# Three early gate/up product groups moved in between the last rows of an out-projection

## The chip, the cores and the metric

The kernel runs on one core of one Trainium2 chip. The metric is the device time of one execution in microseconds (us), smaller is better. Engines are called TensorE (PE in the profile, its weight loads PEld), VectorE (DVE), ScalarE (ACT), GpSimd (POOL) and SyncE (SP, here the queue that issues the DMAs).

## The reference

A bidirectional encoder trunk with two layers of width 1024 over 1040 tokens (1024 and 16 learned ones ahead of them, which are dropped at the end), all in float32. Cut to what matters:

```
for each layer:
    h  = x + hybrid_mixer(rmsnorm(x)) @ w_out      # chunked gated DeltaNet heads and a gated convolution
    g, u = split(rmsnorm(h) @ w_gate_up)           # the gate/up products
    x  = h + (silu(g) * u) @ w_down
return rmsnorm(x)
```

## The kernel before

The data lie transposed, features on the 128 partitions and tokens along the free axis, so a residual of 1024 features is eight "rows" m = 0 to 7 of 128 features. A float32 product is made of three matmuls on values split into a high and a low half (high by high, high by low, low by high). ScalarE makes the high half by a copy (`hi`), VectorE or GpSimd the low one by a subtraction (`lo`). The work is written with a scheduler that fixes the order on each engine from an estimate of durations and from priorities; tiles come from pools with few buffers (raw weights: 2, split weights `whi`/`wlo`: 3; PSUM banks `acc` 3, `f` 2, `b` 2, `a` 1), so an instruction may also wait until a buffer is given back.

Around the change, each layer runs so:

**Out-projection, second part.** `out_part(z, m)` makes row m for one half of the tokens, first z = 0 (the two middle quarters), then z = 1 (the two outer quarters). It loads 256 KB of `w_out` (raw, L129), splits it (L130 on ScalarE, L131), runs 12 matmuls into each of two PSUM banks (L157 to L159), reads each bank out into the residual on VectorE (`add_h`, L905), squares the row for the norm (L949 on ScalarE, L950 adds it to `rstd`), and stores the row (L952 on SyncE, where the store waits for L905).

**The tiles of the FFN.** Gate and up are made by a Strassen-like scheme with seven products of half the size per group f, on sums of the residual over the two token halves. The tiles B11 and B21 hold the normed middle tokens and are ready when the z = 0 rows are. T1, B22, T2, T3 and T4 need the z = 1 rows too: between and behind those rows VectorE makes the sums (L977, L1001) and, with ScalarE, the splits (`t_split`: L964 the high half on ScalarE, L965 the low one on VectorE; `t_split_w`: L177 and L178). T2 and T3 take the place of the tiles that every out-projection matmul reads, and T4 that of a residual row group, whose other half later holds a ring of weights.

**Early products.** Behind the rows, for f = 0 to 3, one loop makes the first products of f, from B11 (into `u`) and, added to it, from B21 (into `g`): two raw loads (L1087, L1088), two weight splits (`w_op`: L1042 on ScalarE, L1043 on GpSimd), matmuls (`prod`: L1060 to L1062), and a copy out of PSUM on ScalarE after each (L1095, L1098). They read only B11 and B21. A product with one of the two is a half group here, and (f, q) names it: q = 0 with B11, q = 1 with B21. In layer 0 a half group has 24 matmuls with 260 columns in two banks, in layer 1 (1024 tokens) 12 with 512 columns in one bank.

**Then** `finish_bc` (L207 to L215) sums the squares over the partitions and makes the norm, and the main loop over f loads the weights (L1278 to L1281), makes their sums on VectorE (L1286 to L1291), and runs the other products: P5 and its readers (L1310), the gate (L1321, L1324), P7 (L1328) and P4 (L1337), to the last factor (L1351 to L1354).

Of the kernel before, what the change touches and what calls it, by code (L numbers as in the profile page):

```python
# [7 lines left out]
F32 = mybir.dt.float32  # L8
F32R = mybir.dt.float32r
BF16 = mybir.dt.bfloat16  # L10
AF = mybir.ActivationFunctionType
ALU = mybir.AluOpType
# [3 lines left out]
KT = 8  # L16
# [13 lines left out]
P_L = 65  # L30
P_N1, P_N2, P_CV, P_SC, P_DN = 0, 8, 16, 52, 64
# [11 lines left out]
def trunk(ctx: ExitStack, tc: tile.TileContext, xT, w_in, w_ba, w_out, w_gu, w_dn,  # L43
          par_d, alog_d, dtb_d, cst_d, eye_d, out):
    nc = tc.nc
    sb = ctx.enter_context(tc.tile_pool(name="sb", bufs=1))
# [5 lines left out]
    def nm(p):  # L52
        cnt[0] += 1
        return f"{p}_{cnt[0]}"

    def big(tag, dt=F32):
        return sb.tile([128, 4, L], dt, tag=tag, name=nm(tag))

    def row(tag, dt=F32, bufs=1):
        return sb.tile([128, L], dt, tag=tag, bufs=bufs, name=nm(tag))  # L60
# [4 lines left out]
    def c4k(tag="c"):  # L65
        return sb.tile([128, L], F32, tag="c", bufs=2, name=nm(tag))

    def bank(tag):
        return psp.tile([128, 512], F32, tag=tag, bufs={"acc": 3, "a": 1, "f": 2, "b": 2}[tag], name=nm("p" + tag))
# [29 lines left out]
    act = nc.scalar.activation  # L99
    tt = nc.vector.tensor_tensor  # L100
    stt = nc.vector.scalar_tensor_tensor
    ts = nc.vector.tensor_scalar
    ptt = nc.gpsimd.tensor_tensor
    dma = nc.sync.dma_start
# [4 lines left out]
    par = sb.tile([128, P_W], F32, name="par")  # L109
# [170 lines left out]
    for l in range(DEPTH):  # L280
        last = l == DEPTH - 1
        X, Y = S[l % 2], S[1 - l % 2]
        pcol = lambda c: par[:, l * P_L + c:l * P_L + c + 1]
# [147 lines left out]
        P0 = [sb.tile([16, 4, 16], F32, tag=f"P0{d}", name=nm("P0")) for d in range(2)]  # L431
# [195 lines left out]
        for pos, i in enumerate(seq):  # L627
# [16 lines left out]
            if pos == 2:  # L644
                g, negG, nGb, negE, gl, bkd = gates()
# [232 lines left out]
        for i, (d, s) in enumerate(order):  # L878
            at_prio(base - 17000 + 4000 * (1 - d) + 400 * s)
            c = s if d == 0 else 8 - s  # L880
# [6 lines left out]
        hb = [big(X[0][0]), big(X[0][1])]  # L887
# [15 lines left out]
        def add_h(m, then=None):  # L903
            def f(ps, n0, n1):
                tt(out=hr[m][:, n0:n1], in0=ps, in1=hr[m][:, n0:n1], op=ALU.add)  # L905
                if then is not None:
                    then(n0, n1)
            return f
# [32 lines left out]
        def out_part(z, m):  # L941
            dense(wload(w_out[l, m, :, 0:4, :], 4), os_, hcut[z], add_h(m), pwide)

            v, sv = half(hr[m][:, o0:L], z), half(ss[:, o0:L], z)
            if m == 0:
                act(out=sv, in_=v, func=AF.Square)
            else:
                sq = c4k("sq")[:, 0:NB].rearrange("p (g e) -> p g e", g=2)
                act(out=sq, in_=v, func=AF.Square)  # L949
                (ptt if z == 1 and m % 2 == 0 else tt)(out=sv, in0=sv, in1=sq, op=ALU.add)  # L950
            for (n0, n1) in hcut[z]:
                dma(hd[m][:, n0:n1], hr[m][:, n0:n1])  # L952
# [3 lines left out]
        def t_tile(tag):  # L956
            t = big(tag, F32R).rearrange("p a (b e) -> p (a b) e", b=2)
            return t[:, 0:4, 0:NB], t[:, 4:8, 0:NB]

        def t_split(T, src, z, k0):  # L960

            hi, lo = (t[:, k0:k0 + 2, :].rearrange("p k (g e) -> p k g e", g=2) for t in T)
            s = half(src[:, k0:k0 + 2, o0:L], z)
            act(out=hi, in_=s, func=AF.Copy)  # L964
            tt(out=lo, in0=s, in1=hi.bitcast(F32), op=ALU.subtract)  # L965

        def hx(k, z):
            return half(hr[k][:, o0:L], z)

        def t_split_w(T, k, z):  # L970

            hi, lo = (t[:, k % 4, :].rearrange("p (g e) -> p g e", g=2) for t in T)
            split_scaled(hx(k, z), pcol(P_N2 + k), hi, lo)

        def t_sum(k, z, src, col, other, op=ALU.subtract):

            stt(out=hx(k, z), in0=src, scalar=col, in1=other, op0=ALU.mult, op1=op)  # L977

        npar = sb.tile([128, 4], F32, tag="npar", name=nm("npar"))
        ts(out=npar, in0=par[:, l * P_L + P_N2:l * P_L + P_N2 + 4], scalar1=-1.0, scalar2=None, op0=ALU.mult)  # L980
        X0, X1 = hb
        T = {}

        for m in range(KT):
            out_part(0, m)
            if m > 0:
                if m in (1, 5):
                    T[("B11", "B21")[m // 4]] = t_tile((Y[0][0], X[0][2])[m // 4])
                t_split_w(T[("B11", "B21")[(m - 1) // 4]], m - 1, 0)
        for m in range(KT + 2):  # L990
            if m < KT:
                out_part(1, m)
            if m == 0:
                t_split_w(T["B21"], 7, 0)
            k = m - 2
            if k < 0:
                continue
            if k < 4:
                if k == 0:
                    T["T1"] = t_tile(Y[0][2])  # L1000
                ts(out=hx(k, 1), in0=hx(k, 1), scalar1=pcol(P_N2 + k), scalar2=None, op0=ALU.mult)  # L1001
                t_sum(k, 0, hx(k, 0), npar[:, k:k + 1], hx(k, 1), ALU.add)
                if k % 2:
                    t_split(T["T1"], X0, 0, k - 1)
            else:
                c = pcol(P_N2 + k)
                if k == 4:
                    T["B22"] = t_tile(Y[0][1])
                t_split_w(T["B22"], k, 1)
                t_sum(k - 4, 1, hx(k, 1), c, hx(k - 4, 1))  # L1010
                t_sum(k, 1, hx(k, 1), c, hx(k - 4, 0))
                t_sum(k, 0, hx(k, 0), c, hx(k, 1))
        T["T2"] = t_tile("P0")
        T["T3"] = t_tile("P1")
        for k in (0, 2):
            t_split(T["T2"], X1, 1, k)
        for k in (0, 2):
            t_split(T["T3"], X0, 1, k)
        T["T4"] = t_tile(X[0][0])
        for k in (0, 2):  # L1020
            t_split(T["T4"], X1, 0, k)


        ad = dram.tile([FT, 128, L], F32, name=nm("ad"))
        ring = [None]
        wn = [0]
# [11 lines left out]
        def w_op(src, early=False):  # L1038
            hi, lo = wslot(early)
            n = src.shape[1]  # L1040
            hi, lo = hi[:, 0:n, :], lo[:, 0:n, :]
            act(out=hi, in_=src, func=AF.Copy)  # L1042
            ptt(out=lo, in0=src, in1=hi.bitcast(F32), op=ALU.subtract)  # L1043
            return hi, lo
# [3 lines left out]
        def pbank():  # L1048
            bn[0] += 1
            return bank(("acc", "f", "acc", "b", "acc", "f", "b", "a")[bn[0] % 8])  # L1050

        CW = E if E * 4 > 1024 else NB
        NJ = NB // CW

        def prod(ps, w, t, j, first, stop=True):
            nk = w[0].shape[1]
            for k in range(nk):
                cs = slice(CW * j, CW * j + CW)
                th, tl = (t[0][k], t[1][k]) if isinstance(t[0], list) else (t[0][:, k, :], t[1][:, k, :])
                mm(ps[:, :CW], w[0][:, k, :], th[:, cs], start=first and k == 0, stop=False, skip_group_check=True)  # L1060
                mm(ps[:, :CW], w[0][:, k, :], tl[:, cs], start=False, stop=False, skip_group_check=True)  # L1061
                mm(ps[:, :CW], w[1][:, k, :], th[:, cs], start=False, stop=stop and k == nk - 1, skip_group_check=True)  # L1062

        def raw4(tag):
            if tag == "raw":
                return wp.tile([128, WK, 128], F32, tag="raw", bufs=2, name=nm("raw"))
            return t2k("rw")

        def part(t, z, j):

            v = half(t[:, o0:L], z)
            return v[:, j, :] if NJ == 2 else v
# [6 lines left out]
        def pin(ps):  # L1079
            return loc(ps, 0)  # L1080


        NE = 4
        early = {}
        for f in range(NE):
            A11, A12 = raw4("raw"), raw4("raw")
            dma(A11, w_gu[l, f, 0, :, 0:4, :])  # L1087
            dma(A12, w_gu[l, f, 0, :, 4:8, :])  # L1088
            w1, w2 = w_op(A11, True), w_op(A12, True)
            g, u = (row(Y[1], F32, 3), row(X[1], F32, 3)) if f < 3 else (row(Y[1] + "f"), c4k())  # L1090
            early[f] = g, u
            ab = [pbank() for j in range(NJ)]
            for j in range(NJ):
                prod(ab[j], w1, T["B11"], j, True)
                act(out=part(u, 0, j), in_=pin(ab[j]), func=AF.Copy)  # L1095
            for j in range(NJ):
                prod(ab[j], w2, T["B21"], j, False)
                act(out=part(g, 0, j), in_=pin(ab[j]), func=AF.Copy)  # L1098

        finish_bc(ss, o0, L, rsd[0])  # L1100

# [149 lines left out]
        for t in range(4, NP * 7):  # L1251
            u = max(0, 4 * (t // 3 - 1) - 1 + t % 3)
# [23 lines left out]
        for f in range(FT):  # L1276
            A11, A12, A21, A22 = raw4("raw"), raw4("raw"), raw4("ck2"), raw4("ck2")
# [20 lines left out]
            g, u = early[f] if f < NE else (row((X[1], Y[1])[f % 2] + "f"), row(X[1], F32, 3))  # L1298
# [65 lines left out]
        hb = [big(X[0][0]), big(X[0][1])]  # L1364
# [38 lines left out]
        for i in range(NF):  # L1403
            u = (42, 44, 46, 70)[i]
            under[u - 3].append(lambda i=i: plain_load(i))
            under[u].append(lambda i=i: plain_row(i))
        for u, (p, b, m) in enumerate(UNITS):
            if b == 1 and p in FIRST:
                dh, z = FIRST[p]
                q = 4 * dh + m  # L1410
# [163 lines left out]
```

## Time and profile before

| | us |
|---|---|
| median of 3 runs | 2555.83 (2554.69 to 2557.81) |
| profiled execution | 2552.45 |
| its span in the trace | 2550.7 |
| mean granted TensorE clock | 0.997 |

All numbers of the trace come from the profiled execution. A row of a timeline gives the start in us from the span's start, the length, the engine, the line and operation, out<-in with tile names (buffer numbers left out), the shape, and in brackets the time for which the engine had been idle ahead of it and what ended that. A row of the table by stretches gives for each engine the busy time within the stretch with the count of instructions, then the TensorE clock that was granted (1.00 is full), the mean busy share of the DMA engines and GB/s. Layer 0 passes the end of its out-projection at about 600 us, layer 1 at about 1863 us.

### The profile page before, as it was taken

The numbers are of one execution on the slowest core, as the hardware profiler recorded it, in microseconds if no ns is written. First come the engines' busy times: TensorE is split into PE (matmuls) and PEld (weight loads), VectorE is DVE, ScalarE is ACT, GpSimd is POOL, SyncE is SP. The second block draws the span as 40 slices with busy tenths as digits, with TensorE's granted clock in tenths as the row PEclk, the third lists the DMA queues.
The fourth block names the chain that finished last, engine by engine and source line by source line (L and its number), as shares of the span: only waits on it lengthen the run. The fifth ranks groups of instructions, "written<-read, shape, count | busy, mean of one in ns | idle before, by whom it ended". The sixth has DMA issues, their size and how long they took to land. (4 is left out here: it accounts for less than half of the span.)

```text
span 2550.7 us, 45276 instructions
## 1 busy us (share of the span) xinstructions
PE 2488.7 (98%) x17508; PEld 2276.4 (89%) x17508; DVE 1613.0 (63%) x2442; ACT 1070.3 (42%) x2053; POOL 1141.9 (45%) x885
## 2 busy tenths in 40 slices
PE   8999999999999999999999999999989999999998
PEld 6989999998999999999999988998968778787787
DVE  4689233748766655778555882236697776559664
ACT  5664333535233333444445642335443333234444
POOL 1141212425666666655320303123457666575662
PEclk9999999999999999999999999999999999999999
DMA  3444354624322332664224534446332233328641
GB/s 129 138 155 146 123 156 132 196 79 130 107 84 98 114 102 94 211 217 139 89 94 130 163 123 144 132 138 204 120 126 95 87 108 107 99 96 280 183 123 67
DMA packets 199531, 335.27 MB, mean 131 GB/s; under 512 B 23404, under 2 KB 85668, under 8 KB 199316
## 3 DMA queue, kind: packets, MB, share of 16 engines
q1 hardware_dynamic: 171204, 293.84, 35.5%
q10 hardware_dynamic: 25936, 34.19, 4.3%
q0 software_dynamic: 2176, 4.36, 0.5%
q8 instruction: 137, 2.24, 0.4%
q14 instruction: 78, 0.64, 0.1%
HBM read 250.31 MB, written 81.99 MB: 130 GB/s over the span
## 5 line engine op out<-in xcount | busy, mean ns | idle before, releaser
L131 POOL TENSOR_TENSOR wlo<-raw,whi 128x512 fp32r<-128x512 f32 x132 | 175.0, 1328 | 633.1 <-ACT whi L130 537.1
L157 PE MATMUL pacc<-a,whi 128*128 128x346 f32 (+1 forms) x808 | 263.6, 329 | 9.6 <-ACT whi L130 6.2
L159 PE MATMUL pacc<-a,wlo 128*128 128x346 f32 (+1 forms) x808 | 262.2, 326 | 0.5 <-DVE wlo L131 0.4
L157 PE MATMUL pacc<-b,whi 128*128 128x346 f32 (+2 forms) x672 | 233.6, 349 | 1.7 <-ACT b L900 1.7
L159 PE MATMUL pacc<-b,wlo 128*128 128x346 f32 (+2 forms) x672 | 232.6, 348 | 0.0
L158 PE MATMUL pacc<-a,whi 128*128 128x346 f32 (+1 forms) x688 | 225.1, 327 | 0.9 <-DVE a L901 0.9
L130 ACT ACTIVATE whi<-raw 128x512 fp32r<-128x512 f32 x168 | 105.3, 630 | 228.6 <-PE pacc L158 109.7
L158 PE MATMUL pacc<-b,whi 128*128 128x346 f32 (+2 forms) x580 | 199.9, 346 | 0.0
L157 PEld LDWEIGHTS pacc<-a,whi 128*128 128x128 f32 x808 | 152.3, 189 | 14.4 <-ACT whi L130 8.0
L1043 POOL TENSOR_TENSOR wlo<-rw,whi 128x512 fp32r<-128x512 f32 x92 | 132.0, 1436 | 73.8 <-ACT whi L1042 68.7
L159 PEld LDWEIGHTS pacc<-a,wlo 128*128 128x128 f32 x808 | 152.5, 189 | 1.8 <-DVE wlo L131 0.5
L157 PEld LDWEIGHTS pacc<-b,whi 128*128 128x128 f32 x672 | 126.4, 188 | 13.4 <-issue 3.1
L158 PEld LDWEIGHTS pacc<-a,whi 128*128 128x128 f32 x688 | 130.1, 189 | 4.9 <-issue 3.4
L159 PEld LDWEIGHTS pacc<-b,wlo 128*128 128x128 f32 x672 | 126.3, 188 | 8.9 <-issue 0.8
L1043 POOL TENSOR_TENSOR a<-rw,a 128x512 fp32r<-128x512 f32 x64 | 103.8, 1623 | 65.7 <-ACT a L1042 62.0
L1043 POOL TENSOR_TENSOR b<-rw,b 128x512 fp32r<-128x512 f32 x64 | 91.5, 1432 | 82.5 <-ACT b L1042 57.1
L1042 ACT ACTIVATE whi<-rw 128x512 fp32r<-128x512 f32 x92 | 57.8, 631 | 147.9 <-DVE rw L1290 68.3
L158 PEld LDWEIGHTS pacc<-b,whi 128*128 128x128 f32 x580 | 109.2, 188 | 7.0 <-issue 0.4
L1286 DVE TENSOR_TENSOR rw<-rw,rw 128x512 f32<-128x512 f32 x44 | 62.4, 1417 | 50.3 <-POOL wlo L1043 25.9
L1042 ACT ACTIVATE b<-rw 128x512 fp32r<-128x512 f32 x64 | 40.1, 630 | 125.8 <-PE pacc L1061 30.9
L1043 POOL TENSOR_TENSOR wlo<-raw,whi 128x512 fp32r<-128x512 f32 x50 | 74.7, 1497 | 36.2 <-ACT whi L1042 32.0
L296 DVE TENSOR_TENSOR a<-pacc,rstd 128x346 f32<-128x346 f32 (+2 forms) x59 | 32.6, 553 | 88.7 <-PE pacc L159 88.6
(973 smaller groups left out, 8452.3 us busy)
## 6 DMA issues: line engine op xcount, KB each, us to landing
raw<-in_w_in SPq DMA_DIRECT2D x112, 256.0 KB, 2.9
raw<-in_w_gu SPq DMA_DIRECT2D x104, 256.0 KB, 2.8
rw<-in_w_gu SPq DMA_DIRECT2D x88, 256.0 KB, 2.6
rw<-in_w_dn SPq DMA_DIRECT2D x94, 192.0 KB, 3.2
rec<-vkd SPq DMA_DIRECT2D x61, 256.0 KB, 3.3
raw<-in_w_out SPq DMA_DIRECT2D x48, 256.0 KB, 2.7
b<-ad SPq DMA_DIRECT2D x45, 260.0 KB, 2.7
a<-ad SPq DMA_DIRECT2D x45, 256.0 KB, 3.0
```

The lines of the kernel that those rows point to most:

```text
L130: whi_done[0] = act(out=hi, in_=raw[:, 0:kk, :], func=AF.Copy)
L131: (tt if lov[0] else ptt)(out=lo, in0=raw[:, 0:kk, :], in1=hi.bitcast(F32), op=ALU.subtract)
L157: mm(ps[:, :n], wh, xh[:, n0:n1], start=(k == 0), stop=False)
L158: mm(ps[:, :n], wh, xl[:, n0:n1], start=False, stop=False)
L159: mm(ps[:, :n], wl, xh[:, n0:n1], start=False, stop=(k == K - 1))
L296: tt(out=t[:, n0:n1], in0=ps, in1=rstd[:, n0:n1], op=ALU.mult)
L1042: act(out=hi, in_=src, func=AF.Copy)
L1043: ptt(out=lo, in0=src, in1=hi.bitcast(F32), op=ALU.subtract)
L1286: tt(out=s1t, in0=A21, in1=A22, op=ALU.add)
```

## The change

The helpers (`wslot`, `w_op`, `pbank`, `prod`, `raw4`, `part`, `loc`, `pin`) move ahead of the z = 1 rows without a change to them. The loop over f becomes a function for one half group, which loads its own weights, one raw load of 256 KB each:

```
+        NE = 4
+        early, bks0 = {}, {}
+
+        def early_part(f, q):
+
+            A = raw4("raw")
+            dma(A, w_gu[l, f, 0, :, 4 * q:4 * q + 4, :])
+            w = w_op(A, True)
+            if q == 0:
+                early[f] = (row(Y[1], F32, 3), row(X[1], F32, 3)) if f < 3 else (row(Y[1] + "f"), c4k())
+                bks0[f] = [pbank() for j in range(NJ)]
+            for j in range(NJ):
+                prod(bks0[f][j], w, T[("B11", "B21")[q]], j, q == 0)
+                act(out=part(early[f][1 - q], 0, j), in_=pin(bks0[f][j]), func=AF.Copy)
...
         for m in range(KT + 2):
             if m < KT:
                 out_part(1, m)
             if m == 0:
                 t_split_w(T["B21"], 7, 0)
+
+            for f, q in {5: [(0, 0)], 6: [(0, 1)], 7: [(1, 0)]}.get(m, ()):
+                early_part(f, q)
...
-        NE = 4
-        early = {}
-        for f in range(NE):
-            A11, A12 = raw4("raw"), raw4("raw")
-            dma(A11, w_gu[l, f, 0, :, 0:4, :])
-            dma(A12, w_gu[l, f, 0, :, 4:8, :])
-            w1, w2 = w_op(A11, True), w_op(A12, True)
-            g, u = (row(Y[1], F32, 3), row(X[1], F32, 3)) if f < 3 else (row(Y[1] + "f"), c4k())
-            early[f] = g, u
-            ab = [pbank() for j in range(NJ)]
-            for j in range(NJ):
-                prod(ab[j], w1, T["B11"], j, True)
-                act(out=part(u, 0, j), in_=pin(ab[j]), func=AF.Copy)
-            for j in range(NJ):
-                prod(ab[j], w2, T["B21"], j, False)
-                act(out=part(g, 0, j), in_=pin(ab[j]), func=AF.Copy)
+        for f, q in ((1, 1), (2, 0), (2, 1), (3, 0), (3, 1)):
+            early_part(f, q)
 
         finish_bc(ss, o0, L, rsd[0])
```

So (0,0) is issued behind row 5, (0,1) behind row 6 and (1,0) behind row 7 of the z = 1 rows, each ahead of that step's sums in the program's text; the other five stay behind the splits of T4. The number of instructions of each kind is the same, and the order on each engine is what the scheduler makes of the new text.

More of the change, by code (lines that the diff above doesn't have):

```diff
@@ L977, in t_sum @@
             stt(out=hx(k, z), in0=src, scalar=col, in1=other, op0=ALU.mult, op1=op)
[L979 to L1021, printed above, removed]
         ad = dram.tile([FT, 128, L], F32, name=nm("ad"))
@@ new lines, in trunk @@
+        npar = sb.tile([128, 4], F32, tag="npar", name=nm("npar"))
+        ts(out=npar, in0=par[:, l * P_L + P_N2:l * P_L + P_N2 + 4], scalar1=-1.0, scalar2=None, op0=ALU.mult)
+        X0, X1 = hb
+        T = {}
+        for m in range(KT):
+            out_part(0, m)
+            if m > 0:
+                if m in (1, 5):
+                    T[("B11", "B21")[m // 4]] = t_tile((Y[0][0], X[0][2])[m // 4])
+                t_split_w(T[("B11", "B21")[(m - 1) // 4]], m - 1, 0)
+        for m in range(KT + 2):
+            if m < KT:
+                out_part(1, m)
+            if m == 0:
+                t_split_w(T["B21"], 7, 0)
+            for f, q in {5: [(0, 0)], 6: [(0, 1)], 7: [(1, 0)]}.get(m, ()):
+                early_part(f, q)
+            k = m - 2
+            if k < 0:
+                continue
+            if k < 4:
+                if k == 0:
+                    T["T1"] = t_tile(Y[0][2])
+                ts(out=hx(k, 1), in0=hx(k, 1), scalar1=pcol(P_N2 + k), scalar2=None, op0=ALU.mult)
+                t_sum(k, 0, hx(k, 0), npar[:, k:k + 1], hx(k, 1), ALU.add)
+                if k % 2:
+                    t_split(T["T1"], X0, 0, k - 1)
+            else:
+                c = pcol(P_N2 + k)
+                if k == 4:
+                    T["B22"] = t_tile(Y[0][1])
+                t_split_w(T["B22"], k, 1)
+                t_sum(k - 4, 1, hx(k, 1), c, hx(k - 4, 1))
+                t_sum(k, 1, hx(k, 1), c, hx(k - 4, 0))
+                t_sum(k, 0, hx(k, 0), c, hx(k, 1))
@@ L1100, in trunk @@
+        T["T2"] = t_tile("P0")
+        T["T3"] = t_tile("P1")
+        for k in (0, 2):
+            t_split(T["T2"], X1, 1, k)
+        for k in (0, 2):
+            t_split(T["T3"], X0, 1, k)
+        T["T4"] = t_tile(X[0][0])
+        for k in (0, 2):
+            t_split(T["T4"], X1, 0, k)
+        for f, q in ((1, 1), (2, 0), (2, 1), (3, 0), (3, 1)):
+            early_part(f, q)
         finish_bc(ss, o0, L, rsd[0])
```

## The prediction

> **What bounds the kernel now.** I read the page's totals first: over the whole span TensorE hardly rests, so a change of order can win only what TensorE loses where the order changes.
>
> ```profile
> PE 2488.7 (98%) x17508; PEld 2276.4 (89%) x17508; DVE 1613.0 (63%) x2442; ACT 1070.3 (42%) x2053; POOL 1141.9 (45%) x885
> ```
>
> Next the busy time by stretches, around the end of the out-projection of layer 0 (590 to 650) and of layer 1 (1860 to 1940). Columns: stretch, length, then PE, PEld, DVE, ACT, POOL busy with their counts, granted clock, DMA share, GB/s.
>
> ```profile
> 590.00:600.00 10.00, 10.00 (x86) 10.00 (x86) 9.68 (x12) 4.42 (x7) 7.23 (x5) 1.00 0.46 147
> 600.00:610.00 10.00, 5.83 (x44) 5.24 (x43) 10.00 (x15) 6.01 (x10) 5.91 (x4) 0.98 0.29 94
> 610.00:620.00 10.00, 10.00 (x73) 10.00 (x73) 10.00 (x10) 6.52 (x13) 4.72 (x4) 0.85 0.32 105
> 620.00:630.00 10.00, 8.72 (x71) 8.30 (x70) 10.00 (x9) 5.25 (x9) 3.02 (x2) 1.00 0.30 93
> 630.00:640.00 10.00, 9.42 (x78) 8.38 (x76) 4.91 (x8) 5.72 (x13) 7.76 (x6) 1.00 0.39 120
> 640.00:650.00 10.00, 8.74 (x70) 8.56 (x71) 8.50 (x12) 3.07 (x4) 6.23 (x6) 1.00 0.55 172
> ...
> 1860.00:1870.00 10.00, 7.59 (x40) 6.51 (x39) 10.00 (x14) 5.51 (x9) 5.97 (x4) 0.83 0.30 92
> 1870.00:1880.00 10.00, 7.36 (x36) 4.69 (x34) 10.00 (x11) 6.26 (x10) 5.79 (x5) 1.00 0.37 118
> 1880.00:1890.00 10.00, 10.00 (x50) 7.66 (x43) 10.00 (x10) 5.65 (x9) 3.66 (x3) 1.00 0.32 107
> ...
> 1910.00:1920.00 10.00, 7.38 (x25) 5.88 (x26) 4.80 (x9) 3.71 (x5) 4.92 (x3) 0.83 0.25 79
> 1920.00:1940.00 20.00, 20.00 (x88) 16.19 (x87) 17.17 (x15) 5.68 (x9) 16.64 (x10) 1.00 0.26 93
> ```
>
> A full stretch holds 86 of the 260-wide matmuls, so one takes 10.00/86 = 0.116 us and a half group of 24 (two banks of 12) 2.8 us. From 600 to 630 there ran 44 + 73 + 71 = 188 instead of 258: 70 x 0.116 = 8.1 us lost. From 630 to 650 there ran 148 instead of 172: 2.8 us. Layer 0 loses 10.9 us here. The same rows show what fills the time: **VectorE is busy 10.00 of 10.00 in every stretch from 600 to 630, and from 1860 to 1890.** TensorE's waits, in the timeline (start, length, engine, line, the idle time before it and what ended it), with the last matmul of the last row of each layer ahead of the first of them:
>
> ```profile
> 601.29 0.28 PE L159 MATMUL pacc<-o,wlo 128*128 128x260 f32 x1
> 602.18 0.36 PE L1060 MATMUL pf<-b,whi 128*128 128x260 f32 x1 [0.62 <-DVE a L905]
> 606.43 0.39 PE L1060 MATMUL pb<-b,whi 128*128 128x260 f32 x1 [1.12 <-ACT whi L1042]
> 609.37 0.39 PE L1060 MATMUL pacc<-b,whi 128*128 128x260 f32 x1 [2.43 <-DVE a L905]
> ...
> 640.00 0.39 PE L1060 MATMUL pacc<-b,whi 128*128 128x260 f32 x1 [0.44 <-DVE a L1310]
> 649.72 0.36 PE L1060 MATMUL pacc<-b,whi 128*128 128x260 f32 x1 [1.26 <-DVE a L1310]
> ...
> 1862.99 0.27 PE L159 MATMUL pf<-o,wlo 128*128 128x256 f32 x1
> 1865.67 0.71 PE L1060 MATMUL pf<-a,whi 128*128 128x512 f32 x1 [2.41 <-DVE b L905]
> 1874.44 0.50 PE L1060 MATMUL pf<-b,whi 128*128 128x512 f32 x1 [0.97 <-ACT b L1095]
> 1879.72 0.64 PE L207 MATMUL pa<-rstd,ones 128*32 128x256 f32 x8 [1.42 <-DVE rstd L950]
> 1893.01 0.50 PE L1062 MATMUL pb<-a,wlo 128*128 128x512 f32 x1 [1.24 <-POOL wlo L1043]
> 1912.62 0.50 PE L1060 MATMUL pa<-P,b 128*128 128x512 f32 x1 [3.11 <-DVE a L1324]
> ```
>
> In layer 1 the five waits make 9.15 us. Two slow-clock stretches (0.83) add 10 x 0.17 = 1.7 us each: 12.5 us. So the ceiling of any gain is 10.9 + 12.5 = 23 us, 0.9% of the run. The large waits are for VectorE to read a PSUM bank out (L905). VectorE itself, in the timeline:
>
> ```profile
> 601.62 0.42 DVE L905 TENSOR_TENSOR a<-pf,a 128x260 f32<-128x260 f32 x1
> ...
> 608.90 0.75 DVE L905 TENSOR_TENSOR a<-pacc,a 128x260 f32<-128x260 f32 x2
> ...
> 611.76 2.44 DVE L977 SCALAR_TENSOR_TENSOR a<-a,par,a 128x520 f32<-128x520 f32 x2
> 614.12 1.42 DVE L178 SCALAR_TENSOR_TENSOR b<-a,par,b 128x520 fp32r<-128x520 f32 x2
> ...
> 626.07 3.48 DVE L965 TENSOR_TENSOR a<-a,a 128x1040 fp32r<-128x1040 f32 x2
> 629.47 0.68 DVE L1287 TENSOR_TENSOR rw<-rw,raw 128x512 f32<-128x512 f32 x1
> 630.07 0.68 DVE L1291 TENSOR_TENSOR rw<-raw,rw 128x512 f32<-128x512 f32 x1
> ...
> 637.52 0.71 DVE L1286 TENSOR_TENSOR rw<-rw,rw 128x512 f32<-128x512 f32 x1 [3.49 <-DMA rw<-in_w_gu]
> ...
> 1871.31 0.41 DVE L905 TENSOR_TENSOR b<-pacc,b 128x256 f32<-128x256 f32 x1
> ...
> 1888.39 3.44 DVE L965 TENSOR_TENSOR b<-b,b 128x1024 fp32r<-128x1024 f32 x2
> ```
>
> L905 of the last row runs at 608.90 although TensorE had ended that row at about 601.4, and in layer 1 at 1871.31 against about 1863.3. VectorE is 7.5 and 8 us behind there. It then works through the sums and splits to T4 (629.5 and 1891.8), which the second product P5 and the weight ring need. So the stretch is bounded by VectorE's chain to T4, and after it by the weights; TensorE's eight half groups only fill it.
>
> **The change part by part.** Counts of all instructions stay the same: nothing is added or removed, three of the eight half groups per layer move ahead of the last rows. So VectorE's work to T4 is the same sum. What can change is whether it waits.
>
> *Layer 0, TensorE.* After row 5 the changed order runs (0,0), row 6, (0,1), row 7, (1,0). Counted back from 601.4 by 2.8 us a row, row 5 ends at 595.7, (0,0) at 598.5, the first bank of row 6 at 600.0. Its second bank is the one that L905 at 601.62 reads out, so it stands until 602.04: a new wait of 2.1 us. Then bank 2 of row 6 (603.5), the two banks of (0,1) around row 7's first (607.8). Row 7's second bank needs row 6's L905, which in the changed order stands four to eight VectorE instructions later: at about 608.5, a wait of 0.75. Row 7 ends at 610.2 instead of 601.4. VectorE reaches row 7's own L905 only after three more L977 (1.22 each by 611.76) and one L178 (0.71 by 614.12) behind 608.90: 608.90 + 0.75 + 3.66 + 0.71 = 614.0. **So there are some 4 us of margin, VectorE doesn't wait, and T4 stays at 629.5.** Two weight sums now stand ahead of the last T4 split: two times 0.68, 1.4 us later.
>
> *The loads.* Three weight loads move forward on SyncE's queue, in among the stores of the residual rows, which wait there for L905. Row 7's weight load takes the place in the queue that an early load had:
>
> ```profile
> 597.34 0.33 SPq L1088 DMA_DIRECT2D raw<-in_w_gu  x1
> ```
>
> Such a load lands 2.7 us after its issue by the page's list of DMA issues:
>
> ```profile
> raw<-in_w_out SPq DMA_DIRECT2D x48, 256.0 KB, 2.7
> ```
>
> That is 600.1, ahead of row 7's first bank (near 605 above). I take no delay; if SyncE's stores hold it longer, it has 4 us, and what goes beyond is rival (b).
>
> *Layer 0, the rest.* ScalarE's last split for T4, from its timeline:
>
> ```profile
> 625.03 1.08 ACT L964 ACTIVATE a<-a 128x1040 fp32r<-128x1040 f32 x1 [0.44 <-DVE a L977]
> ```
>
> From 610.2 the five remaining half groups take 14 us, their weights cost about 1.3 us at the third (of the kind of the 1.12 above), so TensorE comes to P5 near 626. P5's weights stand on ScalarE behind T4's split (ends 626.1), an early weight and two copies, 2 to 3 us in all by the splits of 0.61 below: I take a wait of 2.7. In all about 7 us of waits against 8.1. Behind that, the load of A22 for the next f moves on SyncE ahead of another raw load, so most of the 3.49 us that VectorE waits at 637.52 goes, and with it 0.44 and part of 1.26. I take **-2 us for layer 0** (between -4, if these two and one more us go, and +1, if the 1.4 us passes through and the load brings nothing).
>
> *Layer 1.* The weights of row 7 are split by ScalarE behind the first of these instructions, from its timeline:
>
> ```profile
> 1864.23 1.06 ACT L964 ACTIVATE a<-b 128x1024 fp32r<-128x1024 f32 x1 [4.15 <-DVE b L977]
> 1865.19 0.61 ACT L949 ACTIVATE sq<-b 128x512 f32<-128x512 f32 x1
> ...
> 1866.33 0.61 ACT L1042 ACTIVATE whi<-raw 128x512 fp32r<-128x512 f32 x1
> ```
>
> It waits for L977 on VectorE. Behind it stand, in the changed order too, the square (0.61) and a scaled split, and then row 7's weights (0.61, ready near 1867.0); the next copy and the later weights are queued behind those. TensorE reaches row 7 at about 1863.4: a new wait of 3.4 us in place of 2.41. Row 7 ends near 1874.5 (12 matmuls of 512 columns are 12 x 20.00/88 = 2.7 us), and VectorE reaches its two L905 at about 1874.2 and 1876: margin 0 to 1.5 us, thin. finish_bc (L207) comes near 1881 instead of 1879.72, with TensorE about 1 us ahead. T4 comes 0.6 us later by the two weight sums, and the 3.11 at 1912.62, which hangs on the chain from T4 through the last sums, ends 0.5 later. I take **+0.5 us** (between -1, if the 0.97 and 1.24 go as well, and +3, if the margin is missed by 2 and T4 slips with it).
>
> *Clock.* The waits of 2.43, 2.41 and 3.11 are each followed by a low granted clock (0.85, 0.83, 0.83), worth 10 x 0.15 to 0.17 = 1.5 to 1.7 us. The new waits, 2.1 and 3.4, take the places of the first two; I cost this at nothing, between -3 and +0 (the 2.1 may be short enough). [...]
>
> *Sum:* -2 + 0.5 = -1.5 us. Against the profiled execution's own time, 2552.45 us (span 2550.7), that is 2550.95. The median of the three runs, 2555.83, lies 3.4 above the profiled one, so I predict **2554.3 us**.
>
> **Rivals.** (a) *The idle time is really filled.* For it: 2.43 and 2.41 are waits of TensorE with nothing to do, and three half groups (8.4 us) would fit. Layer 0 would lose the 0.62, 1.12 and 2.43 and 1.5 of clock, and pay 0.75; layer 1 would lose 2.41 with 1.7 and pay 0.5: -4.9 - 3.6 = -8.5, so 2547.3. Against it: VectorE's 10.00 of 10.00. What TensorE gains before T4 it waits at T4, unless VectorE's chain also shrinks.
>
> (b) *The last rows come late, and the run is slower.* Every sum behind T1 needs row 6 and 7. Their weights now queue on ScalarE and SyncE among the early weights. If row 7 passes the margin (4 us in layer 0, 0 to 1.5 in layer 1), VectorE idles and T4, P5 and everything behind slip by the same time. For it: row 7 comes 9 and 11 us later, and the thin margin in layer 1. Against it: VectorE's backlog of 7.5 to 8 us. With a late weight of one ScalarE wait (4.15) beyond the margin of layer 1 and 3 us of layer 0: +7, so 2562.8. It decides from row 7 later than about 614 and 1876.
>
> (c) *The change doesn't do what it says:* the instruction order of the changed kernel excludes it, since (0,0) and (0,1) do stand between the rows in both layers.
>
> **How the numbers follow.** 0.2% of 2555.83 is 5.1 us, about what a measurement of this kernel can tell from no change: 2550.7 to 2560.9 is "same". My forecast's own bounds (-5 to +4 by the layers, the clock's -3 only at its end) lie about in there: 0.50. Rival (a) 0.22, all faster. Rival (b) 0.28, all slower; I give it more than (a) because every error in the walk of ScalarE's queue goes in its direction. The range reaches to just beyond both: 2546 to 2565.
>
> **What would show it.** Right: VectorE still 10.00 of 10.00 from 600 to 630 and 1860 to 1890, T4's last L965 ending near 631 and 1892, TensorE's 2.43 and 2.41 replaced by waits of about 2 us at row 6 (L157 behind L905) and 3.4 us at row 7 (L157 behind ACT L130), and a new wait before P5 in layer 0. (a) would show TensorE without waits over 1 us and T4 earlier; (b) VectorE idle in front of L905 and T4 later than 633 or 1894. The forecast is wrong if the rows' weights come later than ScalarE's queue says, or if ScalarE's copies hold the early banks.

## The result and the profile after

The changed kernel took 2560.49 us (median of 22 runs, 2555.52 to 2565.20) and the kernel before, in the same series, 2556.47 us (2550.73 to 2562.18): a ratio of 1.0017, 95% interval 1.0010 to 1.0023. That is 4 us or 0.17% slower, between 2.6 and 5.9 us, where I had forecast 1.5 us less. It lies inside the 0.2% that I had called "same", but on the other side of it.

The stretches again, with the columns of the table before:

```profile
590.00:600.00 10.00, 10.00 (x85) 10.00 (x85) 9.67 (x13) 4.42 (x7) 7.24 (x5) 1.00 0.48 148
600.00:610.00 10.00, 8.08 (x55) 7.87 (x54) 10.00 (x14) 5.57 (x10) 5.33 (x4) 0.83 0.27 91
610.00:620.00 10.00, 9.21 (x72) 8.58 (x72) 9.93 (x11) 7.07 (x12) 4.38 (x4) 1.00 0.40 112
620.00:630.00 10.00, 7.86 (x64) 7.64 (x64) 9.62 (x9) 6.39 (x13) 4.34 (x3) 1.00 0.25 79
630.00:640.00 10.00, 10.00 (x73) 9.34 (x72) 7.90 (x7) 4.13 (x9) 6.87 (x6) 0.83 0.32 107
640.00:650.00 10.00, 9.11 (x74) 8.72 (x73) 8.08 (x10) 3.70 (x5) 7.59 (x6) 1.00 0.59 192
...
1870.00:1880.00 10.00, 9.17 (x40) 7.89 (x41) 10.00 (x12) 4.77 (x9) 7.26 (x4) 0.67 0.32 106
```

From 600 to 610 TensorE ran 55 matmuls, 11 more than before: the groups did fill the hole. From 620 to 640 it ran 64 + 73 = 137 against 71 + 78 = 149: there the gain went back. Two stretches of layer 0 now have a clock of 0.83, where one had 0.85, and layer 1 has one of 0.67. VectorE stays at 9.6 or more up to 630, nearly the 10.00 that I had forecast.

TensorE's waits in the timeline of the changed kernel:

```profile
602.32 0.39 PE L157 MATMUL pf<-o,whi 128*128 128x260 f32 x1 [1.92 <-DVE a L905]
629.49 0.39 PE L1015 MATMUL pacc<-b,whi 128*128 128x260 f32 x1 [2.14 <-ACT whi L997]
648.57 0.36 PE L1015 MATMUL pacc<-b,whi 128*128 128x260 f32 x1 [0.70 <-DVE a L1314]
651.10 0.39 PE L1015 MATMUL pb<-a,whi 128*128 128x260 f32 x1 [0.60 <-DVE a L1332]
701.20 0.39 PE L1015 MATMUL pacc<-b,whi 128*128 128x260 f32 x1 [1.21 <-DVE a L1314]
...
1870.83 0.58 PE L157 MATMUL pacc<-o,whi 128*128 128x256 f32 x1 [3.44 <-ACT whi L130]
1887.13 0.42 PE L207 MATMUL pa<-rstd,ones 128*32 128x256 f32 x4 [2.01 <-DVE rstd L950]
1917.56 0.80 PE L1015 MATMUL pa<-P,b 128*128 128x512 f32 x1 [3.19 <-DVE a L1328]
```

The three waits that I had walked out are there at their places and nearly in their sizes: 1.92 at row 6 (2.1 forecast), 2.14 ahead of P5 (2.7), 3.44 at row 7 in layer 1 (3.4). What I had not seen is what VectorE does at T4:

```profile
627.12 1.23 DVE L965 TENSOR_TENSOR a<-a,a 128x1040 fp32r<-128x1040 f32 x1
628.27 0.69 DVE L1291 TENSOR_TENSOR rw<-rw,raw 128x512 f32<-128x512 f32 x1
628.88 1.77 DVE L1295 TENSOR_TENSOR rw<-raw,rw 128x512 f32<-128x512 f32 x1
630.57 2.32 DVE L965 TENSOR_TENSOR a<-a,a 128x1040 fp32r<-128x1040 f32 x1
634.95 1.76 DVE L1294 TENSOR_TENSOR rw<-raw,rw 128x512 f32<-128x512 f32 x1 [2.06 <-POOL a L998]
```

T4's last split ends at 632.9, not at 631: the second weight sum ahead of it took 1.77 in place of 0.68 and the split 2.32 in place of 1.23. GpSimd was splitting weights at the same time:

```profile
628.72 1.38 POOL L998 TENSOR_TENSOR wlo<-raw,whi 128x512 fp32r<-128x512 f32 x1 [5.66 <-ACT whi L997]
630.06 1.73 POOL L998 TENSOR_TENSOR wlo<-rw,whi 128x512 fp32r<-128x512 f32 x1
```

In the whole trace of the changed kernel VectorE's 176 weight sums took 0.68 to 0.69 us wherever GpSimd ran nothing beside them (66 of them), and 1.77 in the median where GpSimd was busy throughout (another 66). I had priced both sums by rows with GpSimd idle.

To see where time goes, I count TensorE's matmuls from one point that both traces pass in the same order (592 us in layer 0, 1850 in layer 1) and take how much later the n-th one starts than in the kernel before, less the offset that the two traces have at that point already. Layer 0: 2.9 us **ahead** at the 240th matmul (629 us), 0.7 **behind** at the 288th (635), 0.8 at the 432nd (655), 2.2 at the 1296th (762), and 2.2 still at 800 us. Of the 3.7 us lost from the 240th to the 288th, 2.0 are longer waits (P5's 2.14 above all) and 1.7 a spell behind them: a stretch of 3.4 us at a granted clock of 0.50. Layer 1: 1.2 behind at 1958 us. Together that is 3.4 us, within the measured 2.6 to 5.9. The rest of the traces, which the change doesn't touch, drifts by up to 2 us up and down.

### The profile page after: what moved, and what is told of

The parts are those of the page before. It is cut to its first block, busy times and chain, and to the rows that moved or that the text cites. A ratio compares the mean times of both kernels' runs of the same rounds, so it can differ in the third digit from the quotient of the medians.

```text
span 2557.3 us, 45284 instructions
## 1 busy us (share of the span) xinstructions
PE 2495.2 (98%) x17508; PEld 2283.0 (89%) x17508; DVE 1621.4 (63%) x2442; ACT 1069.8 (42%) x2053; POOL 1145.5 (45%) x885
```

## The experiments

Two theories stood at the start, and a third came after the first runs. **Clock**: the loss is the slow spells behind the new waits, 1.7 us each. **VectorE**: T4 comes 3 us later in each layer, and TensorE waits for what it feeds. **Weights**: the first P5's weights, queued on ScalarE behind T4's split, take the lead back. In all, 18 kernels ran, 6 to 12 runs each. Single runs scatter by some 5 us to either side, so an interval spans 0.2%, about 5 us; the traces are finer: they come to 592 us with offsets of up to 4 us, but with the offset taken off, kernels whose layer 0 runs in the old order (halves, l1only, bfill1) follow the kernel before to 0.2 us. A single trace per kernel stands behind each row. The table gives TensorE's lag in us against the kernel before (minus is ahead) at the 240th, 288th, 432nd and 1296th matmul of layer 0's stretch, at the end of layer 1's, and the ratio of times.

```
kernel      240    288    432   1296  layer 1  ratio, 95% interval
changed    -2.9    0.7    0.8    2.2    1.2    1.0017  1.0010-1.0023
halves      0.0    0.0    0.1    0.1   -0.3    1.0004  0.9996-1.0013
l0only     -3.0    0.7    1.2    2.5   -0.5    1.0004  0.9991-1.0017
l1only      0.0    0.0    0.2    0.2    0.9    1.0006  0.9995-1.0016
one        -3.5    0.8    0.6    4.7    2.5    1.0020  1.0011-1.0030
bank       -2.7    0.1    1.1    5.2    0.3    1.0018  1.0009-1.0027
fill       -2.1    4.6    2.9    2.9    0.7    1.0011  1.0002-1.0021
m6fill     -2.3    1.2    1.8    3.9   -0.2    1.0012  1.0002-1.0021
m6half     -2.8    0.9    1.4    5.1    0.7    1.0020  1.0010-1.0030
p5fill     -2.6    3.6    1.6    4.7    0.3    1.0006  0.9996-1.0016
m6p5fill   -2.2    3.5    3.1    3.0    0.1    1.0001  0.9992-1.0010
p5half     -2.9    1.2    1.0    5.2    0.6    1.0016  1.0005-1.0027
m6p5half   -1.9    3.3    2.2    4.0    0.5    0.9999  0.9989-1.0009
t4first    -3.0    0.8    2.4    5.1    0.3    1.0029  1.0017-1.0041
s1early    -0.7    3.5    2.1    5.2    0.4    1.0017  1.0006-1.0029
s1t4       -0.9    3.6    1.3    2.9    0.8    1.0024  1.0013-1.0035
bfill       1.4    2.1    1.3    1.9   -3.5    1.0008  0.9999-1.0018
bfill1      0.0    0.0    0.2    0.2   -2.7    1.0005  0.9996-1.0014
lite        4.0    3.5    2.1    4.2   -2.4    1.0026  1.0016-1.0036
```

### One part alone: halves, l0only, l1only, one

Each changes only which groups stand between the rows; the others go back to the list behind T4 (the edits are shortened and put side by side here):

```diff
-            for f, q in {5: [(0, 0)], 6: [(0, 1)], 7: [(1, 0)]}.get(m, ()):
+            for f, q in {}.get(m, ()):                                     # halves: none, all eight behind T4
+            for f, q in ([{5: [(0, 0)], 6: [(0, 1)], 7: [(1, 0)]}, {}][l]).get(m, ()):   # l0only (l1only: the other layer)
+            for f, q in {5: [(0, 0)]}.get(m, ()):                          # one: (0,0) alone
```

> Only the loading by halves is kept: all eight half groups stand behind T4 as before, each with its own load. Clock theory and VectorE theory: the time of the kernel before, 2556.5 within 1. If the loading by halves is what costs, 2 to 4 us more than that.

> The move in layer 0 alone, layer 1 as before. By the lag of the changed kernel: 2.2 us behind at the end of layer 0's stretch, nothing in layer 1, and 2 to 3 us over the kernel before in time. If layer 1 were the main cost: within 1 us of the kernel before.

> The move in layer 1 alone, layer 0 as before (by halves). By the lag between the traces layer 1 costs 0.5 to 1.3 us: 0.5 to 1.3 over the kernel before, and layer 0's part of the changed kernel is the rest. If the 3.4 us wait and its double spell at row 7 were the main cost: 3 us over.

> Only (0,0) moves in each layer; the other seven half groups stay behind T4. If each moved group draws its own wait (2 us and a spell): the wait at row 6 goes with the two others, about 1 us over the kernel before. If the walls behind the rows take back whatever lead TensorE has: the same time as before within 1 us, with a lead that is gone by P5.

The loading by halves costs nothing (0.1 us of lag). l0only repeats the changed kernel's layer 0 within 0.4 us, waits and spells included, and l1only its layer 1, with 0.9 where the changed kernel has 1.2 and one spell more (at 1885.2); both as expected, although the times of the two, 1.0004 and 1.0006, can't be told from no change. `one` fell on neither side: its lead of 3.5 is gone by P5, as the walls (waits that take back whatever lead TensorE has) would have it, but it keeps the wait at row 6 and ends 4.7 behind.

### The waits filled: fill, m6fill, m6half, p5fill, m6p5fill, p5half, m6p5half

Matmuls that nothing reads, on operands that have long been there, keep TensorE busy through a wait (shortened):

```diff
+        def keep_busy(n, p=None):
+            p = bank("a") if p is None else p
+            N = CW // 2 if NJ == 1 else CW
+            for i in range(n):
+                mm(p[:, :N], T["B11"][0][:, 0, 0:128], T["B11"][0][:, 0, 0:N], start=True, stop=True, skip_group_check=True)
...
+                keep_busy(16)                  # ahead of row 6's second bank; fill: ahead of row 7 in layer 1 too (28)
...
+                keep_busy(16, ps["c", j])      # ahead of the first P5 (fill 18); p5: pinned behind group (3,0)
                 prod(ps["c", j], W["S1"], T["T1"], j, True)
```

The halves (m6half, p5half, m6p5half) put 8 matmuls in each place.

> The changed kernel with matmuls whose result nothing reads put where TensorE stands: 16 of 260 columns ahead of row 6's second bank and 18 in all ahead of P5 in layer 0, 28 of 256 columns ahead of row 7 in layer 1; 1.9, 2.1 and 3.3 us of work in waits of 1.92, 2.14 and 3.44. Clock theory (the loss is the half-clock spells of 3.4 us that follow the new waits, 1.7 us each): the spells at 603, 631 and 1870 go, some 4 to 6 us less than the changed kernel, about 2555. VectorE theory (T4 comes 3 us later in each layer because two weight sums stand ahead of its last split): no change, about 2560.

> The changed kernel with 16 unread matmuls (1.9 us) only ahead of row 6's second bank, into a PSUM bank that nobody waits for. Clock theory: the spell at 603 goes and the second one stays; 1.7 us less than the changed kernel, in layer 0 a lag of about 0.5 in place of 2.2. If VectorE's chain alone sets the stretch: no change.

> The same with 8 unread matmuls, so that about half of the 1.92 us wait at row 6 stays. No wait up to 1.73 us was followed by a slow spell so far. Clock theory: the spell goes as with 16, 1.7 us less than the changed kernel. If any idle time there draws one: no change.

> The changed kernel with 16 unread matmuls (1.9 us) behind the early group (3,0) and ahead of the first P5 in layer 0, where TensorE waits 2.14 us; row 6's wait and spell stay. If the slow spell behind P5's wait is what turns the lead into a lag: no spell near 631, TensorE 0.8 us ahead of the kernel before at the 290th matmul in place of 0.7 behind, about 1.5 us less than the changed kernel. If the later walls set the lag alone: the same lag of about 2.2 at the end of the stretch.

> The same with 16 unread matmuls at row 6 as well: no spell from 600 to 640. If the spells make the loss, layer 0 ends 0.5 us behind or better. If walls do, 2 to 4 behind as with each alone.

> The changed kernel with 8 unread matmuls (0.95 us) ahead of the first P5 in layer 0; the wait of 2.14 us shrinks to 1.2 and the products behind it keep their order. If the spell behind the wait is what turns the lead into a lag: no spell at 631 and TensorE 0.8 us ahead of the kernel before at the 290th matmul, where the changed kernel is 0.7 behind. If the wall alone does: 0.7 behind again.

> The same with 8 unread matmuls at row 6 as well. If row 6's spell is paid out of the lead that the wall ahead of P5 takes back anyway: the same lag at the 290th matmul as p5half. If it counts: 1.5 us less still.

The spells at the filled waits went, and the lag didn't. (fill and p5fill met another at 636.5 and 635.1, behind new waits of 2.52 and 1.92; in p5fill row 6's wait stayed, 2.10, and drew none.) m6fill has none at 603, and meets P5's wall at nearly the same time with the same wait; on the way it stood for ScalarE's copy (timeline of m6fill, TensorE):

```profile
612.66 0.39 PE L1023 MATMUL pacc<-b,whi 128*128 128x260 f32 x1 [1.48 <-ACT b L1059]
...
629.59 0.39 PE L1023 MATMUL pacc<-b,whi 128*128 128x260 f32 x1 [2.13 <-ACT whi L1005]
```

So row 6's spell is paid out of a lead that TensorE loses anyway. For P5's own spell, p5half is the cleaner test, since fill and p5fill moved the order of the products far more (their 3.6 to 4.6 at the 288th matmul come from waits of 1.9 to 2.5 behind the filling). Its half wait is there, and no spell; the stretch's clock is 1.00:

```profile
629.54 0.39 PE L1015 MATMUL pacc<-b,whi 128*128 128x260 f32 x1 [1.19 <-ACT whi L997]
...
634.46 0.39 PE L1015 MATMUL pacc<-a,whi 128*128 128x260 f32 x1 [1.34 <-ACT c L1052]
```

```profile
626.00:642.00 16.00, 11.63 (x90) 10.17 (x89) 12.08 (x10) 8.63 (x18) 10.10 (x7) 1.00 0.20 68
```

It should have been 0.8 ahead at the 288th matmul, and is 1.2 behind, by the wait of 1.34 for a copy of ScalarE; at the 432nd it is 1.0 behind, the changed kernel 0.8. Its order departs from the changed kernel's from the 270th matmul on, but `one` has p5half's order from the 236th on, with the full wait (2.33) and the spell, and is 0.8 and 0.6 behind at the two places: no more than p5half. **By the lag the clock theory falls for layer 0 up to 655 us:** without the spell TensorE only comes sooner to the next wait. m6p5half fell on neither side of its expectation (3.3 behind at the 288th, in another order). The two kernels with the move and no spell in layer 0's stretch, m6p5fill and m6p5half, end it 3.0 and 4.0 behind. Their times (1.0001 and 0.9999, against 1.0017) are those of the kernel before all the same, as the clock theory would have it; where the rest of the program gave that back I did not find, so by the times the theory is not refuted.

### VectorE's chain to T4: t4first, lite, and bfill

```diff
 t4first (changed kernel; the last line in words)
-            t_split(T["T4"], X1, 0, k)
+            last_t4 = t_split(T["T4"], X1, 0, k)
...
+            if f == 0: the two sums of L1291 and L1295 wait for last_t4

 lite (kernel before), for k = 2 and 3
-                ts(out=hx(k, 1), in0=hx(k, 1), scalar1=pcol(P_N2 + k), scalar2=None, op0=ALU.mult)
+                act(out=hx(k, 1), in_=hx(k, 1), func=AF.Copy, scale=pcol(P_N2 + k))

 bfill (kernel before; bfill1: layer 1 alone)
+                if (l, f, j) in ((0, 1, 1), (1, 0, 0)): keep_busy(18)
                 prod(ab[j], w1, T["B11"], j, True)
```

> The changed kernel with the two weight sums of f = 0 (L1291, L1295) put behind T4's last split on VectorE, as before. VectorE theory: T4 ends 2.5 us earlier in each layer and the time falls by 3 to 5 us, to about 2556. Clock theory: the waits ahead of rows 6 and 7 and their slow spells stay, at most 1 us less, about 2560.

> The kernel before with two of the four scalings of the residual per layer (L1001) on ScalarE in place of VectorE, some 1.2 us each. VectorE theory: T4 ends about 2 us earlier in each layer and the time falls by 2 to 4 us. Clock theory: only what falls away in slow spells, 0 to 3.4 us, and the trace shows them gone where the time fell.

> The kernel before with 18 unread matmuls in each of its two waits of 2.4 us (ahead of the second half bank of the second early group in layer 0, ahead of the first early group in layer 1). Clock theory: the spells at 610 and 1866 go, 1.7 us each, up to 3.4 us less than before, about 2552. VectorE theory: the same time as before, since what TensorE gains it waits at T4.

> The kernel before with 18 unread matmuls ahead of layer 1's first early group alone. If bfill's gain in layer 1 (3 us ahead) stands without its loss in layer 0 (2 us): 2 to 3 us less than the kernel before. If that lead came with the changed layer 0: no difference.

t4first did to VectorE what it was to do (its timeline, offset 2.9 us: T4 ends at 632.1, 629.2 by the clock of the kernel before):

```profile
629.74 2.38 DVE L965 TENSOR_TENSOR a<-a,a 128x1040 fp32r<-128x1040 f32 x2
632.16 1.66 DVE L1291 TENSOR_TENSOR rw<-rw,raw 128x512 f32<-128x512 f32 x1
```

and at the 288th matmul it is 0.8 behind, as the changed kernel is with T4 3 us later. In the end it is slower than the changed kernel, not faster: a wait of 1.86 at 652.70 and its spell take 2.2 us more. In lite (offset 1.4) T4 ends at 627.4, 3.5 us earlier than in the kernel before, and then VectorE stands for a load, and TensorE for the early groups' weights:

```profile
625.02 2.38 DVE L965 TENSOR_TENSOR a<-a,a 128x1040 fp32r<-128x1040 f32 x2
631.19 0.69 DVE L1290 TENSOR_TENSOR rw<-rw,raw 128x512 f32<-128x512 f32 x1 [3.79 <-DMA raw<-in_w_gu]
```

```profile
624.28 0.39 PE L1063 MATMUL pa<-b,whi 128*128 128x260 f32 x1 [3.86 <-ACT whi L1045]
628.58 0.59 PE L1065 MATMUL pa<-b,wlo 128*128 128x260 f32 x1 [3.53 <-POOL wlo L1046]
```

Its ratio is 1.0026. lite is no clean test of T4, since its matmuls run in a new order from the 124th on; t4first, which keeps the changed kernel's order up to the 262nd, is the better one. **So T4 alone isn't the bound either**, which was my reading of VectorE's 10.00 in 10.00: the queue that is always full need not be the one that ends last. bfill's spells at 610 and 1866 went, and its layer 0, in a new order from the 107th matmul on, lost 1.9 by waits for copies and weights. Its layer 1 was 3.5 us ahead, and bfill1's alone 2.7; both gave it back later (the offsets of their traces grow by 6.0 and 6.5 us between 1960 and 2540). No version here beats the kernel before.

### Other waits taken away: bank, s1early, s1t4

```diff
 bank
-        bn = [0]
+        bn = [5]

 s1early (s1t4: with t4first as well): ahead of early group (3,0)
+                A21, A22 = raw4("ck2"), raw4("ck2")
+                dma(A21, w_gu[l, 0, 1, :, 0:4, :])
+                dma(A22, w_gu[l, 0, 1, :, 4:8, :])
+                s1t = raw4("ck2")
+                tt(out=s1t, in0=A21, in1=A22, op=ALU.add)
+                hoisted[0] = A21, A22, s1t, w_op(s1t)
...                                    (the main loop then takes these for f = 0)
```

> The changed kernel with the early products' PSUM banks begun at another place of the list, so that row 6's second bank doesn't wait for row 5 to be read out. Clock theory: the 1.92 us wait at row 6 and its slow spell go, 1.7 us less in layer 0 if no wait takes its place. VectorE theory: TensorE waits for T4 all the same, no change.

> The changed kernel with the weights of the first P5 split ahead of the early group (3,0), so that ScalarE has them ahead of T4's split. Weights theory (layer 0 gives its lead of 2.9 us back at P5, 2.1 in the wait for these weights and the rest in the slow spell behind it): that wait and that spell go, TensorE is 2 us or more ahead of the kernel before at that place, and the run is 2 to 3 us shorter than the changed one. VectorE theory (T4 is 3 us late): the lead is given back at the first product that reads T4, no gain, about 4 us over the kernel before as the changed one.

> Both: these weights early, and the two weight sums behind T4's last split on VectorE. If either theory holds alone, as the better of the two single edits; if P5's weights and T4 late are two walls one behind the other, only this one gains: 3 us or more less than the changed kernel, at or below the kernel before.

bank took away row 6's wait and its spell, and got three others of 1.0 to 1.7 us in its place up to 633; its spell in this stretch came at 706.3, behind a wait of 2.07. s1early cut P5's to 1.57 us, and the next wall is about 5 us behind it, at S2's products (TensorE of s1early, then of s1t4):

```profile
636.47 0.40 PE L1015 MATMUL pb<-P,a 128*128 128x260 f32 x1 [2.75 <-ACT a L997]
```

```profile
637.88 0.59 PE L1015 MATMUL pb<-P,a 128*128 128x260 f32 x1 [2.56 <-ACT a L997]
```

ScalarE's split of S2 ends there, and what it split was late on VectorE, which stood for a load (VectorE of s1early, behind T4's last split at 629.82):

```profile
635.00 0.69 DVE L1303 TENSOR_TENSOR rw<-rw,raw 128x512 f32<-128x512 f32 x1 [2.92 <-DMA raw<-in_w_gu]
```

With T4's sums moved as well (s1t4) that wait stays. The weights theory falls too: P5's wait was only the first wall. The pair also bears on row 6's spell, for their matmuls run in one order: s1early has it and s1t4, with nearly the same wait, has not, and both are 3.5 to 3.6 behind at the 288th.

## Why the prediction was wrong

**The bound.** "The stretch is bounded by VectorE's chain to T4" was half of it. P5 doesn't read T4, against what I wrote: it reads T1 and the split weights S1. Of the weights only those in the ring wait for T4's split, S2 first (ScalarE of the changed kernel, just as that split ends):

```profile
632.92 1.15 ACT L997 ACTIVATE a<-rw 128x512 fp32r<-128x512 f32 x2 [2.94 <-DVE a L965]
```

That TensorE's lead isn't kept is shown by every kernel with the move in layer 0: 0.7 to 3.5 us ahead at the 240th matmul, in none ahead at the 288th. That VectorE's chain alone takes it is not: t4first and lite end it earlier and gain nothing, and in lite and s1early VectorE itself then stands 2.9 to 3.8 us for a raw load. Loads, ScalarE's copies and splits, and VectorE's sums are late one behind the other, and I had priced only the last of these queues.

**The waits in layer 0.** Right in place and size (1.92 and 2.14). Row 7's L905 ran at 613.55 and 616.05 (614.0 forecast) without an idle time of VectorE ahead of it, so rival (b) did not happen, though the result is on its side.

**The gain in layer 0: this step failed.** I took -2 us, and 2.2 was lost. Up to the 432nd matmul (655 us) TensorE's idle times sum to 6.3 us against 7.3 before, so about 1 us of the 2 came, and the second spell took 1.7: hence 0.8 behind. I had put T4 at 631 and the A22 load ahead, so that VectorE's wait of 3.49 at 637.52 would go "and with it 0.44 and part of 1.26". The wait went. But L1294 ran at 634.95 instead of 632.26, for T4's last split ended 3.3 us later (3.1 without the offset of 0.24), where I had allowed 1.4 for the two sums, and TensorE's waits from 640 to 655 are 0.19, 0.70 and 0.60, together 1.5, against 0.44 and 1.26, 1.7 before. So of the 1 us that I had counted on there, 0.2 came. Row 6's and P5's waits and the slow clock behind them took the place of the old ones in full: 191 matmuls from 600 to 630 against 188. The bound of +1 was too near as well: behind the stretch that I had walked out (up to 650) I took nothing, and another 1.4 us were lost by 762, of which longer waits make 0.6 (3.3 us from the 432nd matmul on, against 2.7).

**Layer 1.** +0.5 forecast, 1.2 measured, and -0.2 to 0.9 in the seven other kernels whose layer 1 has the same move and no other edit (m6fill, m6half, p5fill, m6p5fill, p5half, m6p5half, l1only): right in size. The mechanism was only half right, so some of that is luck. finish_bc's result came at 1883.4 by the clock of the kernel before (1887.13 less the offset of 3.7) where I had said 1881, and TensorE stood for it 2.0 us, not 1. By the same clock T4 ended at 1894.7 where I had said 1892 (later than the 1894 that I had named as a sign of rival (b)), again behind a weight sum of 1.79, and row 7's L905 ran at 1875.7 and 1877.5 (1874.2 and 1876 forecast), with no idle time of VectorE ahead of them.

**The clock.** I cost the new waits at nothing, since they "take the places of the first two". But the third wait of my own list, 2.7 ahead of P5, was longer than the 2.43 and 2.41 that had each drawn a dip (to 0.85 and 0.83 over ten us), and I charged it none. In layer 0 there were two spells in place of one, in layer 1 one of 6.8 us in place of 3.4:

```profile
603.40:606.80 3.40, 3.40 (x18) 3.40 (x17) 3.40 (x5) 2.48 (x5) 1.75 (x1) 0.50 0.31 90
630.70:634.10 3.40, 3.40 (x18) 3.40 (x17) 2.19 (x1) 1.18 (x3) 1.55 (x2) 0.50 0.59 190
1869.70:1876.50 6.80, 5.67 (x14) 4.60 (x15) 6.80 (x8) 3.48 (x7) 5.32 (x3) 0.50 0.37 118
```

The count was wrong. By the lags of `one` and p5half the price in layer 0 was near nothing up to 655 us all the same, for another reason than mine: the spells lay in time that TensorE would have waited. The times of m6p5fill and m6p5half leave room for a higher price.

**What stays open.** Why a lag of 0.8 at 655 us becomes 2.2 in the changed kernel and up to 5 in others. Six of them (one, m6fill, m6half, p5fill, p5half, m6p5half) show a further wait of 2.0 us between 671 and 676 for one of VectorE's results, which the changed kernel hasn't. The scheduler writes a new order for the products of f = 0 to 2 in most of the kernels, and the traces tell what follows it. Compared by tile names, the matmuls from the 432nd to the 1296th stand in one order in the changed kernel and l0only, in one and p5half, and in fill and m6p5fill; within each pair the lag grows there by the same, 1.4, 4.1 to 4.2, and -0.1. In two more such pairs it grows by 1.5 more in m6half than in m6fill, and in s1early than in s1t4, and the first of each alone has a spell there (at 674.3 and 703.1). halves, l1only and bfill1 have the order of the kernel before and no lag. So the loss behind P5 goes with the order, and a spell there does cost most of its 1.7 us. Which step of the order makes the rest of it, and why the times of m6p5fill and m6p5half don't show their lags, the runs don't tell.

## What to carry to other kernels

Where TensorE stands in front of several queues that are each nearly late, work moved into its idle time can be idle time moved (here leads of 0.7 to 3.5 us at the 240th matmul, and none at the 288th): ask what the second and third wait behind the removed one are, and price the move by the last of them. An engine that is busy in every slice need not be the bound; shorten its queue in an experiment before building on it. Price every wait that is as long as one that has drawn a slow spell as if it drew one too (in layer 0's stretch here 18 of 24 waits of 1.86 to 2.2 us did). And walk the new order as far as the lag still changes (here 150 us), not up to the end of the edited stretch; where a scheduler rewrites the order, compare only kernels that share it.

## What the runs showed of the hardware

In the stretches above, each slow spell in the traces of the two kernels has a granted clock of 0.50 and lasts 3.41 us (before: from 609.6, 1865.7 and 1913.5; changed: from 603.4, 630.7 and 1917.5) or twice that, 6.83 (changed: from 1869.7). The table's 0.83 are 3.4 us at 0.50 in ten. In layer 0's stretch of the traces here, 18 of 24 waits of 1.86 to 2.2 us were followed by a spell, among them 1.92 and 2.14 above, and none up to 1.73 us. With eight unread matmuls in a wait of 1.92 or 2.14 us no spell followed (m6half, p5half: one trace each, with 0.96 and 1.19 us of the wait left).
